# A decoder block on one core: another order of the beginning, and the state-space tables on VectorE

## The chip, the core and the metric

The kernel runs on one core of one Trainium2 chip. The core's engines work side by side and wait for one another by semaphores: TensorE (PE) multiplies matrices into PSUM, VectorE (DVE) and ScalarE (ACT) do element-wise work, GpSimd (POOL) too, and SyncE (SP) issues most DMA transfers. The metric is the device time of one execution in microseconds (us); lower is better.

## The reference

One layer of a hybrid decoder for 256 positions of 2048 channels, all in float32. What matters here, cut to the core:

```python
h = rms_norm(x, g_mix)
proj = h @ w_in                      # u, z_ssm, c_q, k, v, z_attn, k_idx, w_idx, gate_ssm, gate_attn
# state-space branch: 64 groups of 16 channels, a complex diagonal state of 64 per group
abar = exp(dt * (a_re + i a_im));  bb = f(abar) * b
h_t = abar * h_(t-1) + bb u_t;     y = Re(c h) + d_skip * u        # associative scan over positions
y_ssm = glu(gelu(y) @ w_glu) * silu(z_ssm)
# attention branch: an indexer picks 64 keys per query; attention over those keys
y_attn = attention(q(c_q), k, v, picked) * silu(z_attn)
merged = sigmoid(gate_ssm) * (y_ssm @ w_ssm_out) + sigmoid(gate_attn) * (y_attn @ w_attn_out)
x = x + merged @ w_o;  x = x + sigmoid(rms_norm(x) @ w_ple_gate) * rms_norm(p @ w_ple)
return rms_norm(x, g_final)
```

## The kernel before, in words

**Arithmetic.** Every matrix product is made of three passes on rounded parts. A weight `w` is split into `hi` (a cast on ScalarE, `unit_hi`, L243) and `lo` = `w` - `hi` (a subtraction on VectorE, `unit_lo`, L255); the activation has such parts too (`xgh`, `xgl` for x times the gain). A product is hi·high + hi·low + lo·high (`mm3`, L144), three matmuls for each of the 16 k-tiles of 128 channels.

**Units.** The weights stream from memory in units of 128 x 1024 (512 KB). The list `units` holds them in the order of their use: 16 units for u (8 blocks of two halves, `block_k16`, L280), 16 for z_ssm, 32 for gate_ssm, 16 for z_attn, 24 for gate_attn; unit 104 is the first of the query latent c_q, then come k (112 to 115), v, the query products, and from unit 132 the state-space output. A unit of u has 24 matmuls of 256 columns. `weave` (L296) swaps units 1 and 2, so that the first halves of the first two blocks (k-tiles 0 to 7) come before their second halves. A raw unit has 5 buffers, `hi` and `lo` have 4 each; `hi` of unit k waits until TensorE is done with unit k - 4.

**The step.** One turn of the last loop of `block_kernel` is a step, and its number is that of its unit. Step s emits, in this order: what the unit needs first (`need`), its matmuls, `unit_hi(s + 3)`, evictions that are due (`run_deferred`, L194), `unit_lo(s + 2)`, the load of a later unit (`issue_unit`, L88), and a portion of background work (`pump`, L229).

**Background work.** The tables of the state-space branch, the norm of x, the branch itself and the attention are Python generators (threads). `pump(BUDGET)` adds 1.3 to a credit (at most 3.0) and advances the first thread that is due until the credit is used; a thread names the charge of each piece in its `yield`, and `("lag", n)` lets it rest until n steps later. `drain` (L237) advances a thread to its end without looking at the credit. Threads are served in the order of the list.

- `s5_tables` (L754) builds the tables: `s5_small` (L681) some 60 instructions of 128 x 32, then four complex products of 128 x 1024 on VectorE (12 pieces at 1.14), then on GpSimd seven powers of abar (`s5_powers`, L732, 49 small instructions) and two more complex products (`cmul_g`), for which nothing is charged. Transposes on TensorE follow. It is spawned with lag 3.
- `s5_gen` (L819) is the branch: twice (halves of the channels) inputs by TensorE, then the scan on VectorE (L859, L861, L863, L865, 19 complex products of 4 instructions each, charge (66 + 32 n) / 960 + 0.05 apiece, n = 32 three times, 8 three times, 1 seven times, 7 three times, 31 three times: 41 in all), then outputs by TensorE. It starts when the tables are done. In a complex product L859 and L861 are independent, L863 adds the first to the target, L865 the second to the same target, and the next product reads that target.
- Unit 104 has `need=["s5"]`: `drain` of `s5_gen` ahead of its matmuls.
- `xnorm_gen` (L366) sums the squares of x: products on GpSimd in `xprep` (L364), one square on ScalarE, sums on GpSimd (L368 to L370) and VectorE, then a factor per position (`rstd_cols`, `row_of`) that the evictions of u (`ev_u`, L386) need.

**Who sets the order.** The framework keeps each engine's queue in the order in which it places the instructions: an instruction goes as soon as its inputs and its buffer are ready by the framework's own reckoning, and among the ready ones the one emitted first. On the chip every queue then runs strictly in that order.

**The beginning.** `first_loads` (L112) issues, all on SP's queue: the gains, x k-tiles 0 and 1, half of unit 0, x 2 and 3, the other half, x 4 to 7, unit 1, x 8 to 11, x 12 to 15, units 2 to 4, and the small table of the branch. Eighteen warm-up matmuls follow. `xprep(q)` makes the parts of four k-tiles of x (casts on ScalarE L360, low parts on VectorE L362) and, for q of 0 and 1, their squares on GpSimd; the second half of x is prepared by `late_x` (L396) ahead of unit 2. In `mm3` order the first block goes k-tile by k-tile through all three passes. The evictions of u run one step after their block, those of the first two blocks four steps after.

Of the kernel before, what the change touches and what calls it, by code (L numbers as in the profile page):

```python
# [18 lines left out]
P = 128  # L19
T = 256  # L20
# [8 lines left out]
GA1 = 3  # L29
NC = 4  # L30
CW = 512
NWARM = 18
BUDGET = 1.3
XLAG = 1
ULATE = 4
TRLAG = 2

C_U, C_ZS, C_CQ, C_K, C_V, C_ZA, C_KI, C_GS, C_GA = 0, 1024, 2048, 2560, 2816, 3072, 4096, 4176, 6224
# [6 lines left out]
def block_kernel(ctx: ExitStack, tc: tile.TileContext, A: dict, out: bass.AP):  # L45
# [18 lines left out]
    def slot(tag, shape, dt=F32):  # L64
        return cp.tile(shape, dt, tag=tag, name=nm(tag))
# [22 lines left out]
    def issue_unit(between=None):  # L88
        n = dma_next[0]
        if n >= len(units):  # L90
            return
        c, h, cols = units[n][:3]
        kind, idx = chunks[c]
        r = wp.tile([P, 1024], F32, tag="raw", name=nm("raw"), bufs=5)
        src = (A["wts"][idx] if kind == "w" else A["wvk"][idx])[:, h * cols:(h + 1) * cols]
        q = 2 if between else 1
        for i in range(q):
            s = slice(i * cols // q, (i + 1) * cols // q)
            nc.sync.dma_start(r[:, s], src[:, s])
            if between and i == 0:  # L100
                between()
        raws[n] = r
        dma_next[0] += 1
# [6 lines left out]
    sabc = const("sabc", [P, 3, 32])  # L110

    def first_loads():  # L112
        def xload(k, n):
            nc.sync.dma_start(xT[:, k:k + n, :], A["xT"][:, k:k + n, :])

        nc.sync.dma_start(gains, A["gains"])
        xload(0, 2)
        issue_unit(lambda: xload(2, 2))
        xload(4, 4)
        issue_unit()  # L120
        xload(8, 4)
        xload(12, 4)
        for i in range(3):
            issue_unit()
        nc.sync.dma_start(sabc, A["sabc"])
# [9 lines left out]
    mhalf = const("mhalf", [P, 2])  # L135
    V.memset(mhalf, -0.5)
    first = const("first", [P, 2])
    S.activation(first, mhalf, AF.Copy)


    def mm(o, l, r, start=True, stop=True, **kw):
# [70 lines left out]
    def spawn_first(gen):  # L212
        t = spawn(gen)
        threads.insert(0, threads.pop())
        return t
# [61 lines left out]
    def flush():  # L277
        run_deferred(True)

    def block_k16(act, evac, need=None, need1=None, M=P, acc=None, late=1):  # L280
        st = {}

        def go(h, hi, lo):
            ah, al = act()
            if h == 0:
                st["ps"] = (acc or main_ps)()
            ps = st["ps"]
            for k in range(8):
                kt = 8 * h + k
                mm3(ps[:M, :T], hi[:, k * M:(k + 1) * M], lo[:, k * M:(k + 1) * M], ah[:, kt, :], al[:, kt, :],  # L290
                    kt == 0, kt == 15)
            if h == 1:
                defer(late, lambda: evac(ps))
        return (lambda hi, lo: go(0, hi, lo), need), (lambda hi, lo: go(1, hi, lo), need1)
# [59 lines left out]

    xsq = slot("S2", [P, KT, T])

    def xprep(q):
        r = slice(4 * q, 4 * q + 4)
        for k in range(4 * q, 4 * q + 4):
            S.activation(xgh[:, k, :], xT[:, k, :], AF.Copy, scale=gcol(G_MIX, k))  # L360
        for k in range(4 * q, 4 * q + 4):
            STT(xgl[:, k, :], xT[:, k, :], gcol(G_MIX, k), xgh[:, k, :].bitcast(F32), ALU.mult, ALU.subtract)  # L362
        if q < 2:
            G.tensor_tensor(xsq[:, r, :], xT[:, r, :], xT[:, r, :], ALU.mult)  # L364

    def xnorm_gen():  # L366
        S.activation(xsq[:, 8:16, :], xT[:, 8:16, :], AF.Square)
        G.tensor_tensor(xsq[:, 0:4, :], xsq[:, 0:4, :], xsq[:, 4:8, :], ALU.add)  # L368
        G.tensor_tensor(xsq[:, 8:12, :], xsq[:, 8:12, :], xsq[:, 12:16, :], ALU.add)
        G.tensor_tensor(xsq[:, 0:4, :], xsq[:, 0:4, :], xsq[:, 8:12, :], ALU.add)  # L370
        yield ("lag", XLAG)
        TT(xsq[:, 0:2, :], xsq[:, 0:2, :], xsq[:, 2:4, :], ALU.add)
        TT(xsq[:, 0, :], xsq[:, 0, :], xsq[:, 1, :], ALU.add)
        yield 1.0
        yield ("lag", 1)
        R["col1"] = rstd_cols(xsq[:, 0, :], P, D, "r1")
        yield ("lag", 1)
        R["row1"] = row_of(R["col1"], "row1")
# [14 lines left out]
                R["s5"] = spawn(s5_gen(), 1)  # L393
        return f

    def late_x():  # L396
        xprep(2)
        xprep(3)
        R["xnorm"] = spawn_first(xnorm_gen())

    ua = {}

    def first_acc(nb):
# [4 lines left out]
        return f  # L408

    for nb in range(8):  # L410
        first = nb < 2
        add_chunk(*block_k16(xact, ev_u(nb), need1=[late_x] if nb == 0 else None,
                             acc=first_acc(nb) if first else None, late=ULATE if first else 1))
        if nb == 1:
            weave()

# [315 lines left out]
    def s5_powers():  # L732
        abr, abi = R["abar"][:, 0], R["abar"][:, 1]

        def cmul(i, xr, xi, yr, yi):
            t0, t1 = st_("er"), st_("eq")
            tt = G.tensor_tensor
            tt(t0, xi, yi, ALU.mult)
            tt(t1, xr, yr, ALU.mult)
            tt(pre[:, i], t1, t0, ALU.subtract)  # L740
            tt(t0, xr, yi, ALU.mult)
            tt(t1, xi, yr, ALU.mult)
            tt(psi[:, i, 1], t1, t0, ALU.add)
            G.tensor_scalar(psi[:, i, 0], psi[:, i, 1], -1.0, None, ALU.mult)

        cmul(0, abr, abi, abr, abi)
        for i, a, b in ((1, 0, 0), (2, 1, 0), (3, 1, 1), (4, 3, 3), (5, 4, 3), (6, 4, 4)):
            cmul(i, pre[:, a], psi[:, a, 1], pre[:, b], psi[:, b, 1])

    def bc(ap, n):  # L750
        return ap.unsqueeze(-1).to_broadcast(list(ap.shape) + [n])
# [2 lines left out]
    def s5_tables():  # L754
# [6 lines left out]
        ci = slot("S7", [P, 3, 32, 32])  # L761
        nc.sync.dma_start(ci[:, 0], A["sc"][:, 1])
        yield 0.0
        bb = slot("S1", [P, 2, 32, 2, 32])
# [6 lines left out]
            TT(o, o, ci[:, 1], op)  # L771
            yield 1.14

        def cmul_g(o, xr, xi, yr, yi, op):
            G.tensor_tensor(o, xr, bc(yr, 32), ALU.mult)
            G.tensor_tensor(ci[:, 2], xi, bc(yi, 32), ALU.mult)
            G.tensor_tensor(o, o, ci[:, 2], op)
# [5 lines left out]
        yield from cmul_v(Bi, bi, br, f[:, 0], f[:, 1], ALU.add)  # L783
        yield from cmul_v(bb[:, 0, :, 0, :], Br, Bi, abr, abi, ALU.subtract)
        yield from cmul_v(bb[:, 1, :, 0, :], Bi, Br, abr, abi, ALU.add)
        s5_powers()
        S.activation(ct[:, 1, 0], ci[:, 0], AF.Copy, scale=-1.0)
        cmul_g(ct[:, 0, 1], ct[:, 0, 0], ci[:, 0], abr, abi, ALU.subtract)
        cmul_g(ct[:, 1, 1], ct[:, 0, 0], ct[:, 1, 0], nabi, abr, ALU.add)
        bl = slot("S2", [P, 2, 16, P])  # L790
        yield ("lag", 2)
        for c in range(2):
# [295 lines left out]
    assert sum(1 for c in chunks if c[0] == "w") == NCH, (len(chunks), NCH)  # L1088


    R["s5t"] = spawn(s5_tables(), 3)
    first_loads()
    for i in range(NWARM):
        mm(wps[:, :T], warm[:, :P], warm)
    unit_hi(0)
    xprep(0)
    unit_lo(0)
    xprep(1)
    unit_hi(1)
    unit_lo(1)  # L1100
    unit_hi(2)
    NU = len(units)
    for s in range(NU):
        step[0] = s
# [130 lines left out]
```

## Time and profile before

| | us |
|---|---|
| runs | 813.30, 812.24, 811.18 |
| median | 812.24 |
| the profiled execution, its own time | 811.61 |
| its span in the profile | 809.8 |
| TensorE busy | 783.5 |
| VectorE busy | 575.1 |
| ScalarE busy | 393.9 |
| GpSimd busy | 72.7 |

The profile shows one execution. "Busy" is the time in which an engine executes; matmuls are pipelined, so their durations overlap and a start-to-start distance is what one costs. Line numbers such as L264 are those of the kernel; all matmuls have the helper's line, L142, and are told apart by their tiles (XH and XL are the parts of x, aux and main are PSUM). "Granted clock" is TensorE's, as a share of 2.4 GHz. A wait is named with the instruction or DMA that ended it.

### The profile page before, as it was taken

How to read it: one execution, taken by the hardware profiler on the slowest of the kernel's cores; microseconds unless marked ns; L12 is line 12 of the kernel's file. 1: busy time of each engine (PE TensorE's matmuls, PEld its weight loads, DVE VectorE, ACT ScalarE, POOL GpSimd, SP SyncE). 2: the span in 40 equal slices, each digit the busy share in tenths (PEclk: the TensorE clock that was granted, in tenths of full speed). 3: DMA queues.
4: the chain of work that ended last, by engine and by line, in shares of the span. 5: the costliest groups of instructions: out<-in, count | busy, mean ns of one | idle time of the engine just before them, and what ended most of it. 6: DMA issues, size and time to landing. Idle time of an engine off the chain costs nothing.

```text
span 809.8 us, 12802 instructions
## 1 busy us (share of the span) xinstructions
PE 783.5 (97%) x5020; PEld 676.5 (84%) x5020; DVE 575.1 (71%) x834; ACT 393.9 (49%) x536; POOL 72.7 (9%) x77
## 2 busy tenths in 40 slices
PE   6899999999999999999999999999999999999993
PEld 5899997887999887799999987887887888888882
DVE  6999656999645999664669877666688555556662
ACT  6354544544566454463445474535445444445542
POOL 4369900000000000000000000000000000000000
PEclk7999999999999999999999999999999999999997
DMA  8576854656745655734754546676767665555522
GB/s 288 182 261 193 270 192 141 201 177 210 260 135 176 194 184 182 252 121 129 243 183 156 194 162 226 224 238 199 268 202 236 224 204 185 184 182 181 184 79 104
DMA packets 52061, 158.07 MB, mean 195 GB/s; under 512 B 5920, under 2 KB 12064, under 8 KB 51616
## 3 DMA queue, kind: packets, MB, share of 16 engines
q1 hardware_dynamic: 47392, 150.96, 57.2%
q10 hardware_dynamic: 4608, 6.29, 2.2%
q8 instruction: 39, 0.64, 0.3%
q14 instruction: 22, 0.18, 0.1%
HBM read 147.79 MB, written 8.39 MB: 193 GB/s over the span
## 4 chain that ended last, share of the span: by engine, by line
PE 36%; issue 11%; DMA 1%; DVE 1%; ACT 1%; ACTq 0%; POOLq 0%; POOL 0%; DVEq 0%
PE main L142 33%; PE aux L142 2%; PE aux L150 1%; DMA zld<-za_d 1%; DVE lo L264 0%; ACT hi L252 0%; DMA raw<-in_wts_dram 0%; DVE S L1022 0%; ACT S L1127 0%; ACTq L1230 0%; ACT S L586 0%; DVE t L980 0%; POOLq L1230 0%; POOL r_c L633 0%; ACT S L1023 0%
## 5 line engine op out<-in xcount | busy, mean ns | idle before, releaser
L252 ACT CAST hi<-raw 128x1024 fp32r<-128x1024 f32 (+2 forms) x259 | 266.4, 1031 | 363.7 <-PE main L142 318.3
L264 DVE TENSOR_TENSOR lo<-raw,hi 128x1024 fp32r<-128x1024 f32 (+2 forms) x259 | 316.5, 1225 | 154.6 <-ACT hi L252 154.0
L142 PE MATMUL main<-hi,S 128*128 128x512 f32 x544 | 175.3, 397 | 0.9 <-ACT S L1023 0.9
L142 PE MATMUL main<-hi,XH 128*128 128x512 f32 (+1 forms) x416 | 163.1, 392 | 0.0
L142 PE MATMUL main<-lo,XH 128*128 128x512 f32 (+1 forms) x416 | 162.4, 390 | 0.4 <-DVE lo L264 0.4
L142 PE MATMUL main<-hi,XL 128*128 128x512 f32 (+1 forms) x416 | 161.9, 389 | 0.0
L142 PE MATMUL main<-XH,hi 128*128 128x256 f32 x448 | 127.5, 285 | 0.0
L142 PE MATMUL main<-XH,lo 128*128 128x256 f32 x448 | 126.2, 282 | 0.0
L142 PE MATMUL main<-XL,hi 128*128 128x256 f32 x448 | 126.1, 282 | 0.0
L142 PEld LDWEIGHTS main<-hi,S 128*128 128x128 f32 x544 | 102.2, 188 | 25.2 <-ACT S L1023 1.6
L142 PE MATMUL main<-lo,S 128*128 128x512 f32 x272 | 107.9, 397 | 0.0
L142 PEld LDWEIGHTS main<-lo,XH 128*128 128x128 f32 x416 | 78.1, 188 | 18.8 <-DVE lo L264 1.9
L142 PEld LDWEIGHTS main<-hi,XH 128*128 128x128 f32 x416 | 78.1, 188 | 18.0
L142 PEld LDWEIGHTS main<-hi,XL 128*128 128x128 f32 x416 | 78.1, 188 | 17.3
L142 PEld LDWEIGHTS main<-XH,hi 128*128 128x128 f32 x448 | 84.8, 189 | 0.6
L142 PEld LDWEIGHTS main<-XH,lo 128*128 128x128 f32 x448 | 84.8, 189 | 0.0
L142 PEld LDWEIGHTS main<-XL,hi 128*128 128x128 f32 x448 | 84.7, 189 | 0.0
L142 PE MATMUL main<-S,hi 128*128 128x256 f32 x384 | 69.3, 283 | 0.1
L142 PEld LDWEIGHTS main<-S,hi 128*128 128x128 f32 x384 | 58.9, 188 | 1.7 <-issue 1.0
L142 PEld LDWEIGHTS main<-lo,S 128*128 128x128 f32 x272 | 51.2, 188 | 11.0
L142 PE MATMUL main<-S,lo 128*128 128x256 f32 x192 | 53.8, 280 | 0.0
L142 PEld LDWEIGHTS main<-S,lo 128*128 128x128 f32 x192 | 36.2, 188 | 0.0
(213 smaller groups left out, 687.0 us busy)
## 6 DMA issues: line engine op xcount, KB each, us to landing
raw<-in_wts_dram SPq DMA_DIRECT2D x247, 512.0 KB, 4.0
raw<-in_wvk_dram SPq DMA_DIRECT2D x8, 336.0 KB, 2.9
gs_d<-big ACTq DMA_DIRECT2D x8, 256.0 KB, 3.9
ga_d<-big ACTq DMA_DIRECT2D x8, 256.0 KB, 4.0
big<-gs_d SPq DMA_DIRECT2D x8, 256.0 KB, 4.3
big<-ga_d SPq DMA_DIRECT2D x8, 256.0 KB, 3.8
S<-in_grow_dram SPq DMA_DIRECT2D x2, 1024.0 KB, 7.7
big<-in_xtok_dram SPq DMA_DIRECT2D x8, 256.0 KB, 3.9
```

The lines of the kernel that those rows point to most:

```text
L142: PE.matmul(o, l, r, start=start, stop=stop, **kw)
L150: PE.matmul(o, i, idn, is_transpose=True)
L252: S.copy(hi[:, o], src[:, o])
L264: TT(lo[:, o], src[:, o], his[u][:, o].bitcast(F32), ALU.subtract)
```

## The change

- Loads: the gains and x k-tiles 0 and 1 are issued on ScalarE's queue; the rest of x stays on SP's queue between the weight units. The first activation, which brings the table load with it, is emitted after these loads. Two more weight units are loaded ahead of the loop, so that step s issues unit s + 7 where it issued s + 5.
- Warm-up: 30 matmuls instead of 18.
- Order: the first two blocks run pass by pass (all eight hi·high, then lo·high, then hi·low of a half) instead of k-tile by k-tile. All of x is prepared ahead of the loop. The evictions of the first four blocks wait 6, 5, 3 and 2 steps.
- Squares and sums of x: two squares on ScalarE, four sums on VectorE, as a thread spawned with lag 2. Nothing of it on GpSimd.
- Tables: the powers and the last two complex products run on VectorE, and their pieces are charged (seven at 1.2, six at 1.14); the thread is spawned with lag 7.

```diff
-NWARM = 18
+NWARM = 30
-        nc.sync.dma_start(gains, A["gains"])
-        xload(0, 2)
-        issue_unit(lambda: xload(2, 2))
-        xload(4, 4)
+        nc.scalar.dma_start(gains, A["gains"])
+        xload(nc.scalar, 0, 2)
+        issue_unit(lambda: xload(nc.sync, 2, 2))
+        xload(nc.sync, 4, 4)
         issue_unit()
-        xload(8, 4)
-        xload(12, 4)
+        xload(nc.sync, 8, 4)
+        xload(nc.sync, 12, 4)
...
-            for k in range(8):
+            if split:
+                for i, (w, a) in enumerate(((hi, ah), (lo, ah), (hi, al))):
+                    for k in range(8):
+                        kt = 8 * h + k
+                        mm(ps[:M, :T], w[:, k * M:(k + 1) * M], a[:, kt, :], start=kt == 0 and i == 0,
+                           stop=kt == 15 and i == 2)
+            for k in range(0 if split else 8):
...
-        if q < 2:
-            G.tensor_tensor(xsq[:, r, :], xT[:, r, :], xT[:, r, :], ALU.mult)
     def xnorm_gen():
-        S.activation(xsq[:, 8:16, :], xT[:, 8:16, :], AF.Square)
-        G.tensor_tensor(xsq[:, 0:4, :], xsq[:, 0:4, :], xsq[:, 4:8, :], ALU.add)
-        G.tensor_tensor(xsq[:, 8:12, :], xsq[:, 8:12, :], xsq[:, 12:16, :], ALU.add)
-        G.tensor_tensor(xsq[:, 0:4, :], xsq[:, 0:4, :], xsq[:, 8:12, :], ALU.add)
-        yield ("lag", XLAG)
-        TT(xsq[:, 0:2, :], xsq[:, 0:2, :], xsq[:, 2:4, :], ALU.add)
-        TT(xsq[:, 0, :], xsq[:, 0, :], xsq[:, 1, :], ALU.add)
-        yield 1.0
+        for h in range(2):
+            S.activation(xsq[:, 8 * h:8 * h + 8, :], xT[:, 8 * h:8 * h + 8, :], AF.Square)
+            yield 0.0
+            yield ("lag", 1)
+        for n in (8, 4, 2, 1):
+            TT(xsq[:, 0:n, :], xsq[:, 0:n, :], xsq[:, n:2 * n, :], ALU.add)
+            yield 1.0
...
-        add_chunk(*block_k16(xact, ev_u(nb), need1=[late_x] if nb == 0 else None,
-                             acc=first_acc(nb) if first else None, late=ULATE if first else 1))
+        add_chunk(*block_k16(xact, ev_u(nb), acc=first_acc(nb) if nb < 2 else None,
+                             late=(6, 5, 3, 2)[nb] if nb < 4 else 1, split=nb < 2))
...
-            tt = G.tensor_tensor
+            tt = TT
...
-            G.tensor_scalar(psi[:, i, 0], psi[:, i, 1], -1.0, None, ALU.mult)
+            V.tensor_scalar(psi[:, i, 0], psi[:, i, 1], -1.0, None, ALU.mult)
         cmul(0, abr, abi, abr, abi)
+        yield 1.2
         for i, a, b in ((1, 0, 0), (2, 1, 0), (3, 1, 1), (4, 3, 3), (5, 4, 3), (6, 4, 4)):
             cmul(i, pre[:, a], psi[:, a, 1], pre[:, b], psi[:, b, 1])
+            yield 1.2
...
-        s5_powers()
+        yield from s5_powers()
         S.activation(ct[:, 1, 0], ci[:, 0], AF.Copy, scale=-1.0)
-        cmul_g(ct[:, 0, 1], ct[:, 0, 0], ci[:, 0], abr, abi, ALU.subtract)
-        cmul_g(ct[:, 1, 1], ct[:, 0, 0], ct[:, 1, 0], nabi, abr, ALU.add)
+        yield from cmul_v(ct[:, 0, 1], ct[:, 0, 0], ci[:, 0], abr, abi, ALU.subtract)
+        yield from cmul_v(ct[:, 1, 1], ct[:, 0, 0], ct[:, 1, 0], nabi, abr, ALU.add)
...
-    R["s5t"] = spawn(s5_tables(), 3)
+    R["xnorm"] = spawn(xnorm_gen(), 2)
+    R["s5t"] = spawn(s5_tables(), 7)
     first_loads()
+    S.activation(first, mhalf, AF.Copy)
...
     unit_hi(0)
-    xprep(0)
+    xhi(range(8))
     unit_lo(0)
-    xprep(1)
+    xlo(range(8))
     unit_hi(1)
     unit_lo(1)
     unit_hi(2)
+    xhi(range(8, 16))
+    xlo(range(8, 16))
+    for i in range(2):
+        issue_unit()
```

`xhi` and `xlo` are the casts and the low parts that `xprep` held.

## Rows read from the trace of the kernel before

**Rows 1.** The page's part 1: busy us, share of span, instructions.
```profile
PE 783.5 (97%) x5020; PEld 676.5 (84%) x5020; DVE 575.1 (71%) x834; ACT 393.9 (49%) x536; POOL 72.7 (9%) x77
```

**Rows 2.** Stretches: length, busy us by engine, clock, DMA share, GB/s.
```profile
35.00:100.00 65.00, 65.00 (x555) 65.00 (x554) 55.73 (x99) 32.40 (x41) 51.33 (x56) 1.00 0.78 249
345.00:797.00 452.00, 450.53 (x2482) 384.26 (x2482) 295.69 (x437) 221.88 (x324) 5.44 (x8) 1.00 0.58 188
```

**Rows 3.** The same for TensorE alone: three stretches of the beginning.
```profile
5.50:34.30 28.80, 20.26 (x120) 0.76 0.69 239
24.45:27.50 3.05, 0.00 (x0) 1.00 0.02 3
27.50:32.30 4.80, 4.78 (x27) 0.64 0.64 201
```

**Rows 4.** Timeline, SP and ScalarE: start, us, operation [idle before, releaser].
```profile
3.06 0.43 SPq L114 DMA_DIRECT2D S<-in_xT_dram  x1
...
9.30 0.62 ACT L252 CAST hi<-raw 128x512 fp32r<-128x512 f32 x1 [2.17 <-DMA raw<-in_wts_dram]
...
10.55 1.70 ACT L360 ACTIVATE XH<-S,gains 128x256 fp32r<-128x256 f32 x4 [0.63 <-DMA S<-in_xT_dram]
```

**Rows 5.** All engines in a stretch, columns as in rows 2.
```profile
10.00:15.00 5.00, 1.74 (x5) 1.01 (x4) 4.56 (x3) 4.45 (x11) 4.31 (x2) 0.50 1.01 392
```

**Rows 6.** Timeline, VectorE and GpSimd in the beginning.
```profile
10.59 1.89 POOL L364 TENSOR_TENSOR S<-S 128x1024 f32<-128x1024 f32 x1 [2.22 <-DMA S<-in_xT_dram]
...
11.09 4.97 DVE L362 SCALAR_TENSOR_TENSOR XL<-S,gains,XH 128x256 fp32r<-128x256 f32 x4 [0.44 <-ACT XH L360]
...
17.19 3.24 DVE L362 SCALAR_TENSOR_TENSOR XL<-S,gains,XH 128x256 fp32r<-128x256 f32 x8
...
19.40 4.51 POOL L369 TENSOR_TENSOR S<-S 128x1024 f32<-128x1024 f32 x1 [4.42 <-ACT S L367]
...
24.08 4.52 DVE L264 TENSOR_TENSOR lo<-raw,hi 128x1024 fp32r<-128x1024 f32 x2
```

**Rows 7.** Timeline, TensorE in the beginning.
```profile
1.04 4.02 PE L142 MATMUL main<-warm 128*128 128x256 bf16 x18 [1.04 <-DVE mhalf L136]
...
8.71 0.58 PE L142 MATMUL aux<-XL,hi 128*128 128x256 f32 x1 [1.17 <-DVE XL L362]
```

**Rows 8.** Timeline, GpSimd at the start, VectorE in the first scan.
```profile
0.86 0.95 POOL L805 MEMSET kb<- 128x1024 f32 x1
...
133.99 1.22 DVE L863 TENSOR_TENSOR S<-S,S 128x1024 f32<-128x1024 f32 x1
135.13 1.22 DVE L264 TENSOR_TENSOR lo<-raw,hi 128x1024 fp32r<-128x1024 f32 x1
136.27 1.22 DVE L865 TENSOR_TENSOR S<-S,S 128x1024 f32<-128x1024 f32 x1
137.41 1.23 DVE L264 TENSOR_TENSOR lo<-raw,hi 128x1024 fp32r<-128x1024 f32 x1
```

**Rows 9.** VectorE alone in a stretch of the second scan.
```profile
294.54:331.89 37.35, 36.84 (x58) 1.00 0.58 191
```

**Rows 10.** Groups by form, VectorE, 294.54:331.79: busy us, mean ns, idle.
```profile
L264 DVE TENSOR_TENSOR lo<-raw,hi 128x1024 fp32r<-128x1024 f32 x12 | 14.7, 1221 | 0.0
...
L859 DVE TENSOR_TENSOR S<-S,pre 128x992 f32<-128x992 f32 x3 | 3.6, 1189 | 0.0
...
L859 DVE TENSOR_TENSOR S<-S,pre 128x224 f32<-128x224 f32 x3 | 1.7, 570 | 0.0
```

**Rows 11.** Groups by form, VectorE, 348 to 372 us, query-latent evictions.
```profile
L448 DVE SCALAR_TENSOR_TENSOR S<-t,gains,S 128x256 fp32r<-128x256 f32 x4 | 1.9, 479 | 0.0
L441 DVE TENSOR_TENSOR t<-main,row 128x256 f32<-128x256 f32 x4 | 1.7, 425 | 1.9 <-PE main L142 1.9
L450 DVE TENSOR_TENSOR acc<-acc,t 128x256 f32<-128x256 f32 x3 | 1.3, 418 | 0.0
```

**Rows 12.** Timeline, ScalarE at the start of unit 89.
```profile
294.54 1.05 ACT L252 CAST hi<-raw 128x1024 fp32r<-128x1024 f32 x1 [1.02 <-PE main L142]
```

More of the change, by code (lines that the diff above doesn't have):

```diff
@@ L31 @@
 CW = 512
-NWARM = 18
+NWARM = 30
 BUDGET = 1.3
-XLAG = 1
-ULATE = 4
 TRLAG = 2
@@ L112, in first_loads, with xload @@
     def first_loads():
-        def xload(k, n):
-            nc.sync.dma_start(xT[:, k:k + n, :], A["xT"][:, k:k + n, :])
-        nc.sync.dma_start(gains, A["gains"])
-        xload(0, 2)
-        issue_unit(lambda: xload(2, 2))
-        xload(4, 4)
+        def xload(q, k, n):
+            q.dma_start(xT[:, k:k + n, :], A["xT"][:, k:k + n, :])
+        nc.scalar.dma_start(gains, A["gains"])
+        xload(nc.scalar, 0, 2)
+        issue_unit(lambda: xload(nc.sync, 2, 2))
+        xload(nc.sync, 4, 4)
         issue_unit()
-        xload(8, 4)
-        xload(12, 4)
+        xload(nc.sync, 8, 4)
+        xload(nc.sync, 12, 4)
         for i in range(3):
@@ L137, in block_kernel @@
     first = const("first", [P, 2])
-    S.activation(first, mhalf, AF.Copy)
     def mm(o, l, r, start=True, stop=True, **kw):
@@ L278, in flush, with block_k16 @@
         run_deferred(True)
-    def block_k16(act, evac, need=None, need1=None, M=P, acc=None, late=1):
+    def block_k16(act, evac, need=None, need1=None, M=P, acc=None, late=1, split=False):
         st = {}
@@ L355, in block_kernel, with xhi, xlo @@
     xsq = slot("S2", [P, KT, T])
-    def xprep(q):
-        r = slice(4 * q, 4 * q + 4)
-        for k in range(4 * q, 4 * q + 4):
+    def xhi(ks):
+        for k in ks:
             S.activation(xgh[:, k, :], xT[:, k, :], AF.Copy, scale=gcol(G_MIX, k))
-        for k in range(4 * q, 4 * q + 4):
+    def xlo(ks):
+        for k in ks:
             STT(xgl[:, k, :], xT[:, k, :], gcol(G_MIX, k), xgh[:, k, :].bitcast(F32), ALU.mult, ALU.subtract)
-        if q < 2:
-            G.tensor_tensor(xsq[:, r, :], xT[:, r, :], xT[:, r, :], ALU.mult)
     def xnorm_gen():
-        S.activation(xsq[:, 8:16, :], xT[:, 8:16, :], AF.Square)
-        G.tensor_tensor(xsq[:, 0:4, :], xsq[:, 0:4, :], xsq[:, 4:8, :], ALU.add)
-        G.tensor_tensor(xsq[:, 8:12, :], xsq[:, 8:12, :], xsq[:, 12:16, :], ALU.add)
-        G.tensor_tensor(xsq[:, 0:4, :], xsq[:, 0:4, :], xsq[:, 8:12, :], ALU.add)
-        yield ("lag", XLAG)
-        TT(xsq[:, 0:2, :], xsq[:, 0:2, :], xsq[:, 2:4, :], ALU.add)
-        TT(xsq[:, 0, :], xsq[:, 0, :], xsq[:, 1, :], ALU.add)
-        yield 1.0
+        for h in range(2):
[5 more added lines that the diff above has]
+            yield 1.0
         yield ("lag", 1)
@@ L394, in ev_u @@
         return f
[L396 to L399, printed above, removed]
     ua = {}
@@ L410, in block_kernel @@
     for nb in range(8):
-        first = nb < 2
-        add_chunk(*block_k16(xact, ev_u(nb), need1=[late_x] if nb == 0 else None,
-                             acc=first_acc(nb) if first else None, late=ULATE if first else 1))
+        add_chunk(*block_k16(xact, ev_u(nb), acc=first_acc(nb) if nb < 2 else None,
+                             late=(6, 5, 3, 2)[nb] if nb < 4 else 1, split=nb < 2))
         if nb == 1:
@@ L760, in s5_tables @@
         nc.sync.dma_start(ct[:, 0, 0], A["sc"][:, 0])
-        ci = slot("S7", [P, 3, 32, 32])
+        ci = slot("S7", [P, 2, 32, 32])
         nc.sync.dma_start(ci[:, 0], A["sc"][:, 1])
@@ L772, in cmul_v @@
             yield 1.14
[L774 to L777, printed above, removed]
         br, bi = bp[:, 0], bp[:, 1]
```

## The prediction

> **What bounds the kernel now.** I read the page's busy times first, then a table of busy time by stretch, then the order of work where TensorE stands still. TensorE is busy 783.5 of 809.8 us [rows 1], and behind the first 35 us it has next to no hole [rows 2]: 65.0 of 65.0 us and 450.5 of 452 us. So that engine sets the end, and there are two ways to move it: the time it loses before 35 us, and any new hole after it. Idle time of the other engines is worth nothing by itself.
>
> How much is lost in the beginning is read from the count. From 35 to 100 us 555 matmuls take 65 us [rows 2], 0.117 us each, so a weight unit (24 of them) takes 2.81 us. Between 5.5 and 34.3 us there are 120 matmuls, five units, 14.0 us of work in 28.8 us [rows 3]. Three things make up the 14.8 us: waits for the first blocks, a hole of 3.05 us at 24.45, and after it 4.8 us in which 27 matmuls ran at a mean granted clock of 0.64, 1.6 us more than 27 x 0.117.
>
> **The change part by part, first the beginning.**
> Loads: the fourth x load (k-tiles 4 to 7) was issued at 3.06 us, and its casts start at 10.55 when it has landed [rows 4]. Gains and the first x load go to ScalarE's queue, two issues of 0.43 us [rows 4] and their spacing, 0.9 us, fewer ahead of it, so it can land at 9.6 at the earliest, and at 10.55 if only the engines count, which are 1.01 busy at 392 GB/s from 10 to 15 us [rows 5]. I take 10.1. The Trainium skill (Trainium Kernel Development and Optimization, Key Constraints) says that loads of the SP and the ACT queue share the same 16 engines and that a second issuer saves issue time alone; by it, and the busy engines of that row agree, the landing stays nearer to 10.55, and the sum would lose about half a microsecond of its gain. ScalarE has nothing to do before the first x load lands, so its two issues and the later table load are costed at nothing; without that cover they would cost their own 0.9 us.
>
> Squares on GpSimd: the low parts of x on VectorE (L362) take 4.97 us for four while GpSimd squares beside them, and 3.24 us for eight without; two weight splits (L264) take 4.52 us beside GpSimd's sums, the first from 19.40 on [rows 6], where one takes 1.22 us undisturbed [rows 10]. That makes 1.24 against 0.41 us for one low part. All GpSimd work of the beginning is gone, so VectorE follows ScalarE at once. The squares go to ScalarE (two of 2048 columns, at most 8 x 0.425 = 3.4 us each) and the sums to VectorE (15 x 256 columns, some 4.6 us by the 1.22 us of a 1024-wide split, [rows 10]), from step 2 on; the row factor is asked for only in step 8, and the splits run some units ahead of TensorE, so I cost them at nothing; if that cover is gone they cost their own 4.6 us.
>
> Order by pass: the first eight matmuls of a block need no low part of x, so the two first units wait only for casts. ScalarE: casts of k-tiles 4 to 7 from 10.1, four at 0.425 (1.70 for four, [rows 4]), to 11.8. Then 16 matmuls of unit 0 and 24 of unit 1 are free. The warm-up of 30 takes 30 x 0.22 us (18 took 4.02) to about 7.7 us; the first real matmul of before came earlier, but could not go on. A wait of 1.17 us was enough in before to drop the clock: the matmul at 8.71 takes 0.58 us [rows 7]. I therefore take the first 3 us at half speed, 14 matmuls, and the other 26 at 0.117: 11.8 + 3.0 + 3.0 = 17.8 us for two units. Unit 2 needs the low parts of k-tiles 8 to 15 and its own split: ScalarE needs 1.05 + 3.4 + 1.05 us more after 11.8 (a unit's cast takes 1.05, [rows 12]) and VectorE 0.6 for half a split: 17.9, so 18.0. Units 2 to 4 follow without a hole: 18.0 + 8.4 = 26.4 us, where before has 34.3. **Gain 7.9 us**; 5.0 if all 40 matmuls run at half speed, 9.6 if none does.
>
> **The second part of the change is not in the beginning: the table work moved to VectorE delays the scan.** The planner charges background work by the step, 1.3 per unit. Counting its charges from the code: the tables start in step 7 instead of 3, and the seven power products (1.2 each) and six wide operations (1.14 each) that GpSimd did are now charged, 15.2 or twelve steps. The first half of the scan starts in step 50 instead of 35, the second in step 91 instead of 76 (its TensorE inputs stand in steps 87 to 90, and TensorE keeps its order). At step 104 the first query-latent unit demands that the branch is finished (its drain). Before, 39 of the second scan's 41 charge units were given out by then; now about 20 are. The rest is emitted at once, ahead of everything younger.
>
> What is that rest on the chip? Unit 89 of before, 15 steps back, starts at 294.54, where TensorE frees a weight buffer for ScalarE [rows 12]. From there to the scan's end at 331.9 VectorE is 36.8 of 37.35 us busy [rows 9], with 12 weight splits [rows 10] that start 1.14 us apart from what follows them [rows 8]. The scan's share is 37.3 - 12 x 1.14 = 23.6 us. So when TensorE starts unit 104, VectorE has 23.6 us of scan that now ranks above the splits of unit 106 and later. And it stands in a stage with VectorE evictions (0.42 + 0.48 + 0.42 us per two units, [rows 11]), where the gate units of before had none.
>
> Strict rank would starve TensorE: units 104 and 105 take 5.6 us, then it waits to 23.6, a loss of 18.0 us. But rank decides only among what is ready: the memset of L805, emitted in step 28, ran at 0.86 us, and the split of unit 39 (emitted in step 37) stands between the scan's L863 and its older L865 of step 36, the split of unit 40 behind that [rows 8]. Each product of the scan has two such gaps, behind L863 and behind L865. If n splits get in before the scan ends, with c us of evictions, the hole is 23.6 + 1.14 n + c - 2.81 (n + 2). The rest holds three products 224 wide, three 992 wide [rows 10] and narrower ones. In the narrow ones (10 us) the gaps are dense, and units 106 to 109 get their splits as fast as buffers come free. The three wide ones last 13 us and have six gaps; waiting for them are the splits and three evictions per two units, the latter older; I give two gaps to splits. n = 6, and five evictions of 0.42 make c = 2: 23.6 + 6.8 + 2.0 - 22.5 = 9.9 us. After it the clock must rise again, 1.6 us as behind the hole at 24.45 [rows 3]. **Loss 11.5 us**, between 0.6 (n = 12) and 19.6 (n = 0). Then the queue is empty, and the branch's results are not read before unit 132.
>
> The moved table work's own time on VectorE (about 15 us of charges) and the later queue position of SP's other loads (two units more ahead of them) meet a TensorE that is some units behind its buffers; zero to 2 us, I take zero.
>
> **Sum** against the profiled execution's 811.61 us, 0.63 below the median: 811.6 - 7.9 + 11.5 = 815.2 us.
>
> **The rivals.**
> 1. The gaps let nearly all splits through (n of 10 or more, loss 0.6 to 4 us): 811.6 - 7.9 + 2.5 = 806.2 us, faster. For it: both gaps of the product at 134 us were used [rows 8], and 12 splits got in between 294.5 and 331.9 [rows 10]. Against it: most of those 12 outranked the scan, and now evictions compete for the gaps. It decides when n reaches 9 or so.
> 2. Strict rank, no gap used: 811.6 - 7.9 + 19.6 = 823.3 us. Against it [rows 8].
> 3. The beginning gains only 5.0, because the clock stays at half for both first units and loads land no earlier: 818.1 us. For it: the mean clock from 5.5 to 34.3 us was 0.76 [rows 3]; against it: no stop of GpSimd's making is left after 11.8 us.
> 4. The beginning does all it can and the hole stays smaller: 811.6 - 9.6 + 8 = 810 us, no change.
>
> **How the numbers follow.** A measurement of this kernel can tell about 0.3% (2.4 us) from no change. Forecast case 0.52, its own range 811 to 819 (0.37 slower, 0.14 within, 0.01 faster); rival 1 0.27 (0.23 faster, 0.04 within); rival 2 0.09 and rival 3 0.07, both slower; rival 4 0.05, within. Together 0.24 faster, 0.23 within, 0.53 slower. The range leaves out the ends of rivals 1 and 2: 804.5 to 822.
>
> **What would show it.** In the profile of after: unit 4's last matmul near 26 us, no hole at 24; the low parts of x at 0.41 us each; the second scan's first instruction some 34 us later than before's (42 by steps less 8); several splits queued behind the scan's 992-wide instructions, and TensorE holes six or seven units behind unit 104 (between 340 and 370 us) that end on a weight split, about 10 us in all, with the clock at half behind them. If TensorE has no such hole, the step about rank and gaps was wrong and the time is near 805; if unit 4 ends past 29 us, the step on the clock was.

## The result and the profile after

The kernel after takes 823.35 us (median of four, 822.84 to 823.95) where before takes 812.77 (four, 811.18 to 813.96): ratio 1.0132 [1.0111, 1.0152], slower. Its profiled execution has 823.03 us, 11.4 more than the one of before (811.61). The forecast was 815.2 us (804.5 to 822): the side was right, the time lies beyond the range. A time called a single run has no interval; the runs of the kernel before range from 809.8 to 814.7 us.

The page's part 1 of after, against [rows 1]:

```profile
PE 784.9 (96%) x5032; PEld 677.6 (83%) x5032; DVE 575.3 (70%) x891; ACT 391.5 (48%) x534; POOL 8.4 (1%) x17
```

TensorE is as busy as before in a span 11.2 us longer. Where it stands is told by a table of TensorE alone by stretch, whose columns are those of [rows 3]:

```profile
5.50:26.00 20.50, 18.37 (x127) 0.92 0.88 320
300.00:340.00 40.00, 40.00 (x224) 1.00 0.57 185
340.00:380.00 40.00, 21.56 (x301) 0.74 0.23 67
359.25:366.70 7.45, 7.45 (x200) 0.80 0.30 90
370.88:375.92 5.04, 5.04 (x23) 0.50 0.00 0
```

127 matmuls are in by 26 us, where before had 120 by 34.3 [rows 3]; between 340 and 380 us nearly half of the time is lost, and the two short stretches in it, of which more below, ran at a granted clock of 0.80 and 0.50. The waits of TensorE (what it waited for: us in total, times, longest) name two pieces:

```profile
PE aux L139 <- DVE S L857: 14.3, 1, 14.3
PE main L139 <- DVE t L436: 4.2, 1, 4.2
```

L857 is the last addition of a product of the scan (before: L865), L436 the first step of a query-latent eviction (before: L441). The timeline of TensorE there (start, us, operation, idle before and its releaser):

```profile
327.78 0.28 PE L139 MATMUL main<-XH,hi 128*128 128x256 f32 x1
...
344.71 0.28 PE L139 MATMUL main<-XH,lo 128*128 128x256 f32 x1
359.25 1.08 PE L139 MATMUL aux<-S,S 128*32 128x128 f32 x16 [14.26 <-DVE S L857]
...
370.88 0.55 PE L139 MATMUL main<-XH,hi 128*128 128x256 f32 x1 [4.17 <-DVE t L436]
371.22 0.42 PE L139 MATMUL main<-XL,hi 128*128 128x256 f32 x1
...
375.92 0.29 PE L139 MATMUL main<-XH,lo 128*128 128x256 f32 x1
376.05 0.28 PE L139 MATMUL main<-XH,hi 128*128 128x256 f32 x1
```

And VectorE's at the same place (lines left out between):

```profile
329.18 1.22 DVE L261 TENSOR_TENSOR lo<-raw,hi 128x1024 fp32r<-128x1024 f32 x1
...
345.70 1.22 DVE L261 TENSOR_TENSOR lo<-raw,hi 128x1024 fp32r<-128x1024 f32 x1
...
351.25 1.21 DVE L261 TENSOR_TENSOR lo<-raw,hi 128x1024 fp32r<-128x1024 f32 x1
...
356.79 1.21 DVE L261 TENSOR_TENSOR lo<-raw,hi 128x1024 fp32r<-128x1024 f32 x1
357.92 1.18 DVE L857 TENSOR_TENSOR S<-S,S 128x992 f32<-128x992 f32 x1
359.03 1.21 DVE L261 TENSOR_TENSOR lo<-raw,hi 128x1024 fp32r<-128x1024 f32 x1
...
366.79 1.26 DVE L890 SCALAR_TENSOR_TENSOR t<-S,gains,aux 128x256 f32<-128x256 f32 x3 [6.55 <-PE aux L139]
...
370.31 0.75 DVE L436 TENSOR_TENSOR t<-main,row 128x256 f32<-128x256 f32 x2
```

Weight splits (L261) did get in between the scan's instructions: seven from 329.18 to 356.79. No eviction did: the first runs at 370.31, behind the branch's output multiplications (L890). So TensorE finished units 104 to 109 (from 327.78 to 344.99 us), three blocks in the three main PSUM buffers, had no buffer for a fourth, and next in its queue stood the branch's output matmuls, which need the scan's end (357.92 + 1.18 = 359.10). From 346.9 us on it was not a split that it lacked: by the order of units those that start at 345.70 and 351.25 are of units 110 and 111, and neither unit ran.

The account of the 11.4 us. ScalarE's rows show when TensorE was done with the last gate unit, 103, in after:

```profile
327.98 0.69 ACT L425 ACTIVATE big<-main,r_c 128x512 f32<-128x512 f32 x1 [0.71 <-PE main L139]
```

and in before:

```profile
337.13 0.69 ACT L430 ACTIVATE big<-main,r_c 128x512 f32<-128x512 f32 x1 [0.72 <-PE main L142]
```

The beginning is worth 9.15 us, and it is still there. Against it stand the waits of 14.26 and 4.17, 2.3 us because the 23 distances from 370.88 to 375.92 are 0.219 instead of 0.118 us (granted clock 0.50), and 1.1 because the branch's outputs take 7.4 us (359.25 to 366.70, clock 0.80), of which before needed 6.3 at full clock beside a stall of 1.59. That stall, for which the profile shows no releaser, is gone in after, and why is open. 14.3 + 4.2 + 2.3 + 1.1 - 1.6 - 9.15 = 11.1 of 11.4 us.

### The profile page after: what moved, and what is told of

It reads as the page before. It is cut to its first block, busy times and chain, and to the rows that moved or that the text cites. A ratio compares the mean times of both kernels' runs of the same rounds, so it can differ in the third digit from the quotient of the medians.

```text
span 821.0 us, 12810 instructions
## 1 busy us (share of the span) xinstructions
PE 784.9 (96%) x5032; PEld 677.6 (83%) x5032; DVE 575.3 (70%) x891; ACT 391.5 (48%) x534; POOL 8.4 (1%) x17
## 4 chain that ended last, share of the span: by engine, by line
PE 36%; issue 11%; DMA 1%; DVE 1%; ACT 1%; ACTq 0%; POOLq 0%; POOL 0%; DVEq 0%
PE main L139 33%; PE aux L139 2%; PE aux L147 1%; DMA zld<-za_d 1%; DVE lo L261 0%; ACT hi L249 0%; DMA raw<-in_wts_dram 0%; DVE S L1014 0%; ACT S L1125 0%; ACTq L1228 0%; ACT S L581 0%; DVE t L972 0%; POOLq L1228 0%; POOL r_c L628 0%; ACT S L1015 0%
## 5 line engine op out<-in xcount | busy, mean ns | idle before, releaser
L261 DVE TENSOR_TENSOR lo<-raw,hi 128x1024 fp32r<-128x1024 f32 (+2 forms) x259 | 310.2, 1200 | 177.8 <-ACT hi L249 177.6
```

What stands on the lines that cost most here:

```text
L261: TT(lo[:, o], src[:, o], his[u][:, o].bitcast(F32), ALU.subtract)
```

## The experiments

Two theories stood against each other for the loss: the **count of steps** (charged table pieces and a later start delay the scan, and the drain at unit 104 finds its rest open) and the **engine** (VectorE has some 15 us more to do). A third, the **slots**, is about the size of the hole: the branch's output tiles (yv, yf, L889 and L891) share the tag "t" with its 9 buffers with the evictions' temporaries, and the slots of a tag go out in the order of emission, so an eviction emitted behind the drained outputs waits for theirs.

**The slots.** The outputs get a tag of their own:

```diff
-                yv = etmp("t", bufs=9)
+                yv = etmp("ty", bufs=4)
-                yf = etmp("t", bufs=9)
+                yf = etmp("ty", bufs=4)
```

and every other `etmp("t", bufs=9)` becomes `bufs=5`.

> Kernel after, with one edit: the eight output tiles of the state-space branch (yv, yf) get a tag of their own, 'ty' with 4 buffers, and 't', which they shared with the evictions' temporaries, has 5 instead of 9; the number of steps by which the scan is late stays. Theory (slots): in the kernel after, the query-latent evictions did not run before the branch's outputs because they take slots of the same tag behind them in program order. Then here the first query-latent eviction (t L436) starts ahead of the branch's output multiplication (L890), inside the scan, the main PSUM buffers come free one by one, TensorE's wait of 14.3 us at 344.9 on the scan's last instruction becomes shorter, by what the prediction gave for splits and evictions in the gaps (9.9 us hole), and the time is some 813 to 817 us. Rival (rank): the evictions are held back by the scan's older instructions whatever their slots; then t L436 still starts behind 366 us and the time stays at 823.

814.43 us, ratio 1.0024 [1.0014, 1.0035] to before. VectorE's and TensorE's timelines in this kernel:

```profile
341.45 0.46 DVE L436 TENSOR_TENSOR t<-main,row 128x256 f32<-128x256 f32 x1
...
351.51 0.47 DVE L436 TENSOR_TENSOR t<-main,row 128x256 f32<-128x256 f32 x1
```

```profile
352.13 0.55 PE L139 MATMUL main<-XH,hi 128*128 128x256 f32 x1 [5.44 <-DVE t L436]
...
357.58 0.58 PE L139 MATMUL main<-XH,lo 128*128 128x256 f32 x1 [4.68 <-DVE lo L261]
```

The evictions moved into the gaps of the scan, and the 18.4 us of waits became 5.44 + 4.68 + 0.35. Shown: in the kernel after it was the shared tag that held the evictions back, not the scan's older rank. With it out of the way the hole has the forecast's size (10.5 for 9.9 us), but only its second part ends on a weight split; the first, 5.44 us, ends on an eviction, which frees a PSUM buffer.

**The count against the engine.** The table work stays on VectorE, uncharged and started at step 3:

```diff
-        yield 1.2
+        yield 0.0
...
-            yield 1.2
+            yield 0.0
-        yield from cmul_v(ct[:, 0, 1], ct[:, 0, 0], ci[:, 0], abr, abi, ALU.subtract)
+        for _ in cmul_v(ct[:, 0, 1], ct[:, 0, 0], ci[:, 0], abr, abi, ALU.subtract):
+            pass
...
-    R["s5t"] = spawn(s5_tables(), 7)
+    R["s5t"] = spawn(s5_tables(), 3)
```

> Kernel after, with the table arithmetic still on VectorE, but given out in one go without a charge in the planner (as GpSimd's was in the kernel before) and the tables started at step 3 instead of 7. The scan then starts at the steps it had in the kernel before, 15 steps earlier than in the kernel after. Theory (count of steps): what cost the time is only that the scan's rest is still open when TensorE starts unit 104; so there is no hole behind unit 109, and the gain of the beginning stays: 823.4 less about 20 us (14.3 and 4.2 us of waits, some 3 of clock, less the 1.6 us of issue idle that the kernel before had), 803 to 805 us. Rival (engine): VectorE's load grew by some 15 us by the table work and this makes the scan late, however the steps are counted; then the hole stays at more than 8 us and the time above 812.

802.74 us, ratio 0.9884 [0.9861, 0.9907]: faster than both kernels. There is no hole; the longest wait of TensorE behind the warm-up is 0.9 us, and in the stretch in which after lost 18.4 us it is busy throughout:

```profile
340.00:380.00 40.00, 40.00 (x323) 1.00 0.50 149
```

The second scan starts at 257.18 us, 35.3 us or some twelve and a half units ahead of after's (292.52), not the fifteen steps that were expected: the sums of squares on VectorE are still charged at 4.0 instead of 1.0, which at 1.3 a step is 2.3 steps (worked out, not tried), and these do no harm. The reverse puts the arithmetic back on GpSimd and keeps charges and start:

```diff
-            tt = TT
+            tt = G.tensor_tensor
...
+        def cmul_g(o, xr, xi, yr, yi, op):
+            G.tensor_tensor(o, xr, bc(yr, 32), ALU.mult)
+            yield 1.14
...
-        yield from cmul_v(ct[:, 0, 1], ct[:, 0, 0], ci[:, 0], abr, abi, ALU.subtract)
+        yield from cmul_g(ct[:, 0, 1], ct[:, 0, 0], ci[:, 0], abr, abi, ALU.subtract)
...
```

> Kernel after, with the table arithmetic (powers and the two complex products) back on GpSimd, while the charges in the planner and the start at step 7 stay as in the kernel after. It is the reverse of the run without charges. Theory (count of steps): the scan is as late as in the kernel after, TensorE stands some 14 us behind unit 109, and the time is 821 to 825 us. Rival (engine): VectorE is relieved of about 15 us of work, the hole closes to less than 6 us and the time is below 812.

831.6 us (a single run). TensorE's waits here:

```profile
PE aux L139 <- DVE S L865: 14.3, 1, 14.3
PE main L139 <- DVE t L436: 4.2, 1, 4.2
PE main L139 <- DVE lo L261: 4.0, 4, 2.6
```

The two waits of after are there to the tenth (L865 is the last addition in this kernel), with VectorE relieved: the count decides, the engine theory falls. The 8.2 us above after were in no theory (821 to 825 us was the forecast). They lie between 26 and 100 us, where TensorE is busy 70.11 of 74.00 us at a mean granted clock of 0.95 (74.00 at 1.00 in after): a split waits beside GpSimd's 1024-wide products, as the two engines' timelines show:

```profile
78.88 3.37 POOL L776 TENSOR_TENSOR S<-S,S 128x1024 f32<-128x1024 f32 x1
```

```profile
79.93 3.40 DVE L261 TENSOR_TENSOR lo<-raw,hi 128x1024 fp32r<-128x1024 f32 x1
```

The rule of the Trainium skill (SBUF — State Buffer, Who interferes with whom) is that a VectorE instruction with two SBUF inputs and a GpSimd instruction that reads SBUF exclude each other, the later one standing until the earlier is through. The split ends 1.1 us after GpSimd's product, about one split's own time, so the rows agree.

**The size of the delay.** Tables started five steps later:

```diff
-    R["s5t"] = spawn(s5_tables(), 7)
+    R["s5t"] = spawn(s5_tables(), 12)
```

> Kernel after, with the tables started at step 12 instead of 7: five steps later, nothing else. Theory (count of steps): the scan's open rest at unit 104 grows by five steps of 1.3 charge units, 6.5 units, which were about 1.03 us each (23.6 us for 22.3 to 23 units), so TensorE's wait of 14.3 us on the scan grows to about 21 us and the time to 829 to 831 us. Rival: what TensorE waits for behind unit 109 does not scale with the start of the tables; then the time stays within 2 us of 823.

832.67 us (a single run), and of TensorE's waits:

```profile
PE aux L139 <- DVE S L857: 23.4, 1, 23.4
```

That is 9.1 us more than in after, where 6.5 charge units were to give about 7. The direction holds; the price by the unit does not. The scan starts 14.0 us later (306.55 instead of 292.52, five steps), but it ends only 9.2 us later (368.26 instead of 359.10), since it takes 61.7 us instead of 66.6: 14 splits stand between its instructions instead of 18. So a delay of the scan in this stage cost its time less the splits that were then done ahead of it, not its charges.

**The drain.** The branch is demanded at unit 112 instead of 104:

```diff
-        add_chunk(*block_k16(xact, ev_cq(nb), need=["s5"] if nb == 0 else None))
+        add_chunk(*block_k16(xact, ev_cq(nb)))
-        add_chunk(*block_k16(xact, ev_k(nb)))
+        add_chunk(*block_k16(xact, ev_k(nb), need=["s5"] if nb == 0 else None))
```

> Kernel after, with the drain of the state-space branch moved from unit 104 to unit 112: the first key unit demands it, no longer the first query-latent unit. Nothing is charged or started otherwise, so the scan has the same 15 steps of delay. Theory (drain and slots): by unit 112 eight more steps of 1.3 have been given out, so that some 15 of the 25.5 charge units are open, and the query-latent evictions are emitted ahead of the branch's outputs, so they take their slots first and run in the gaps of the scan. Then TensorE's waits behind unit 109 are below 5 us and the time is 804 to 812 us, with the same work on VectorE. Rival (the delay itself costs): TensorE has to stand until the scan's last instruction at 359 us wherever the drain is; then some 8 to 14 us of wait stay and the time is 815 to 823.

809.41 us, ratio 0.9965 [0.9951, 0.9979]. The waits are 6.3 us (0.86, 1.89 and 3.55), a little more than expected, all on weight parts; the first query-latent eviction runs inside the scan, with the tag still shared:

```profile
339.49 0.42 DVE L436 TENSOR_TENSOR t<-main,row 128x256 f32<-128x256 f32 x1
```

The scan is as late as in after (it starts at 293.20 and ends at 365.37), so the delay alone does not set the loss: where the drain stands, and with it what is emitted behind the outputs, does.

**Each part alone.** First the tables' part on top of before:

```diff
-            tt = G.tensor_tensor
+            tt = TT
...
-        s5_powers()
+        yield from s5_powers()
-        cmul_g(ct[:, 0, 1], ct[:, 0, 0], ci[:, 0], abr, abi, ALU.subtract)
+        yield from cmul_v(ct[:, 0, 1], ct[:, 0, 0], ci[:, 0], abr, abi, ALU.subtract)
...
-    R["s5t"] = spawn(s5_tables(), 3)
+    R["s5t"] = spawn(s5_tables(), 7)
```

> Kernel before, with the part of the tables alone (arithmetic on VectorE, charged, start at step 7), and the beginning of the kernel before. Theory (two independent parts): the scan is as late by steps as in the kernel after, the hole behind unit 109 is the same 14.3 and 4.2 us, and nothing is gained in the beginning: 812.6 + some 20 = 831 to 834 us. Rival (the parts interact): the earlier beginning of the kernel after had itself moved TensorE closer to the scan; with a TensorE that comes 9 us later the hole is 5 to 9 us shorter and the time 823 to 827.

831.98 us (a single run), with the two waits of after (L867 and L441 are the lines here):

```profile
PE aux L142 <- DVE S L867: 14.3, 1, 14.3
PE main L142 <- DVE t L441: 4.2, 1, 4.2
```

The beginning has no share in the hole; a later TensorE does not shorten it, since the scan is placed by steps and moves with it: it starts 35.3 us ahead of unit 104 here (300.18 and 335.44) as in after (292.52 and 327.78). The other way round, the kernel after with these lines as they were before:

> Kernel before, with the beginning of the kernel after and the tables as they were before (GpSimd, without charge, start at step 3). Theory (two independent parts): no hole behind unit 109, the gain of 9 us of the beginning stays: 803 to 805 us. Rival (GpSimd beside VectorE): in the kernel with the charged tables on GpSimd a weight split beside GpSimd took 2.8 to 3.4 us instead of 1.23 and TensorE lost 4 us between 26 and 100 us; if that also holds without charges, TensorE waits for low parts there and the time is 806 to 810.

803.1 us, ratio 0.9884 [0.9861, 0.9906]. The whole gain stays without the tables' part, and GpSimd's uncharged products cost nothing that the time shows, although single splits take up to 2.81 us there too; why the same products cost 8.2 us when they are charged is open. The parts add up within the noise: -9.6 and +19.3 give +9.7 of the 10.6 measured.

**Which part of the beginning.** On top of the uncharged kernel (802.74), one part undone at a time. The squares and first sums of x on GpSimd again:

```diff
-        for h in range(2):
-            S.activation(xsq[:, 8 * h:8 * h + 8, :], xT[:, 8 * h:8 * h + 8, :], AF.Square)
-            yield 0.0
-            yield ("lag", 1)
-        for n in (8, 4, 2, 1):
+        S.activation(xsq[:, 8:16, :], xT[:, 8:16, :], AF.Square)
+        yield 0.0
+        yield ("lag", 1)
+        G.tensor_tensor(xsq[:, 0:4, :], xsq[:, 0:4, :], xsq[:, 4:8, :], ALU.add)
+        G.tensor_tensor(xsq[:, 8:12, :], xsq[:, 8:12, :], xsq[:, 12:16, :], ALU.add)
+        G.tensor_tensor(xsq[:, 0:4, :], xsq[:, 0:4, :], xsq[:, 8:12, :], ALU.add)
+        yield ("lag", 1)
+        for n in (2, 1):
...
     xhi(range(8))
+    for r in (slice(0, 4), slice(4, 8)):
+        G.tensor_tensor(xsq[:, r, :], xT[:, r, :], xT[:, r, :], ALU.mult)
```

> Base is the kernel with the uncharged tables on VectorE (802.7 us). One part of the beginning is undone: the squares of x's k-tiles 0 to 7 and the first sums of squares run on GpSimd again. Theory (GpSimd beside VectorE): while GpSimd squares, one low part of x takes 1.24 instead of 0.41 us, and splits beside its sums take more than 2 us, as in the kernel before; the low parts of k-tiles 2 to 7 take up to 5 us longer, unit 0's last pass starts 3 to 5 us later, and the time is 805 to 808 us. Rival: the low parts are ahead of TensorE by enough to hide it, time within 1 us of 802.7.

815.02 us, ratio 1.0017 [0.9998, 1.0036]: no faster than before, and 7 us beyond the upper end of what was expected. VectorE's and GpSimd's timelines:

```profile
7.18 3.70 DVE L366 SCALAR_TENSOR_TENSOR XL<-S,gains,XH 128x256 fp32r<-128x256 f32 x2 [1.52 <-ACT XH L362]
10.80 2.85 DVE L261 TENSOR_TENSOR lo<-raw,hi 128x512 fp32r<-128x512 f32 x1
...
17.15 7.50 DVE L366 SCALAR_TENSOR_TENSOR XL<-S,gains,XH 128x256 fp32r<-128x256 f32 x8
```

```profile
6.62 1.89 POOL L1097 TENSOR_TENSOR S<-S 128x1024 f32<-128x1024 f32 x1 [4.47 <-DMA S<-in_xT_dram]
8.70 1.89 POOL L1097 TENSOR_TENSOR S<-S 128x1024 f32<-128x1024 f32 x1 [0.19 <-DMA S<-in_xT_dram]
10.68 2.42 POOL L372 TENSOR_TENSOR S<-S 128x1024 f32<-128x1024 f32 x1
```

In after two low parts take 0.88 us, a half split 0.69. Here they take 3.70 and 2.85 and end 0.3 and 0.55 us, about their own time, behind the ends of GpSimd's instructions (10.59, 13.10). The cast that waits for unit 4 starts at 34.7 us instead of 25.5. So five GpSimd instructions, put back, take away the whole gain of 9.2 with all other parts of the beginning in place; the other 3 us of the 12.3 are mostly a stall of 2.64 us among the branch's output matmuls (0.31 in the base), whose releaser the profile doesn't show, and which stays open.

The gains and the first x load on SP's queue again:

```diff
-        nc.scalar.dma_start(gains, A["gains"])
-        xload(nc.scalar, 0, 2)
+        nc.sync.dma_start(gains, A["gains"])
+        xload(nc.sync, 0, 2)
```

> Base is the kernel with the uncharged tables on VectorE (802.7 us). One part of the beginning is undone: gains and the first x load are issued on SP's queue ahead of the others again, none on ScalarE's. Theory: every later load on SP is issued 0.9 us later, k-tiles 4 to 7 land up to 1 us later than in the kernel after (8.7 us), unit 0's first pass ends up to 1 us later, and the time is 0.5 to 1.5 us longer: 803 to 804.5. Rival: the landing of the x loads is set by the transfers and not by their issue, or TensorE waits at that point for the low parts anyway: time within 0.4 us of 802.7.

804.08 us, ratio 0.9897 [0.9871, 0.9924]. Unit 0's second pass starts at 11.76 us instead of 10.93 and unit 1 at 15.17 instead of 13.82: this part is worth 1.3 us, as the times say too. Eighteen warm-up matmuls again:

```diff
-NWARM = 30
+NWARM = 18
```

> Base is the kernel with the uncharged tables on VectorE (802.7 us). One part of the beginning is undone: 18 warm-up matmuls instead of 30. They then end near 4 us instead of 6 to 7, TensorE stands some 2.9 us until the first block at 6.9. Theory: the clock is granted at half when the first passes run, so that the 24 matmuls of unit 0 take 0.21 us each until it rises; unit 1 starts up to 2 us later and the time is 803.5 to 805 us. Rival: unit 0's passes wait for casts and low parts anyway and the clock rises in them as it does with 30: within 0.5 us of 802.7.

802.91 us, ratio 0.9884 [0.9852, 0.9916]: no difference to the base. TensorE waits 2.01 us for the first block and then has eight matmuls every 0.95 us from 13.84 on, as with thirty (13.82). What TensorE's clock did in both is told in the last section. The first two units k-tile by k-tile again:

```diff
-                             late=(6, 5, 3, 2)[nb] if nb < 4 else 1, split=nb < 2))
+                             late=(6, 5, 3, 2)[nb] if nb < 4 else 1, split=False))
```

> Base is the kernel with the uncharged tables on VectorE (802.7 us). One part of the beginning is undone: the first two units go k-tile by k-tile again, three products each, instead of pass by pass. Theory: the order by pass lets TensorE run its first matmuls (6.88 to 10.9 us) before low parts of x are there; without it unit 0 starts when the first low part stands, near 11 us, ends between 14 and 16 instead of 13.8, and the time is 0 to 2.5 us longer, plus up to 1 us for a clock that rises later: 803 to 806 us. Rival: the order by pass is what carries most of the beginning's gain; then the time is above 808.

> The kernel of b_order (uncharged tables on VectorE, the first two units k-tile by k-tile), now timed against the kernel before, since one look put it at 801.65 us where its base had 802.74 (802.33 to 803.8). Theory (the order by pass earns nothing): the low parts of x follow the casts so closely once GpSimd is silent that k-by-k gives TensorE its work as early; the clock need not fall in the wait for k-tiles 2 to 7 that the order by pass has after two matmuls; 801 to 802.5 us, faster than all kernels so far. Rival: the one look was a lucky clock; 802.5 to 804 us, and the order by pass is neutral.

801.65 us in a single run, where 803 to 806 was expected; 802.31 as the median of four (802.09 to 802.57, ratio 0.9869 [0.985, 0.9888]), the lowest of all kernels, though its range overlaps that of its base (802.33 to 803.8): the order by pass earns nothing. Unit 0 does not wait until 11 us: it starts at 6.92 and unit 1 at 11.61, since once GpSimd is silent the low parts follow the casts closely enough. TensorE in this kernel and, below it, in the base:

```profile
9.80:13.00 3.20, 3.20 (x26) 1.00 1.01 410
```

```profile
9.80:13.00 3.20, 3.20 (x13) 0.50 1.03 417
```

K-tile by k-tile twice the matmuls run in this stretch, but TensorE then waits 1.2 us for unit 2's cast, and unit 4 ends at 25.17 us instead of 25.42.

## Why the prediction was wrong

**The beginning held, a little better than costed:** 9.15 us by the end of the gate units for 7.9 [rows 3]. Unit 4's end came at 25.7, not 26.4; low parts take 0.41 us each, as taken from their eight in [rows 6]. K-tiles 4 to 7 landed earlier than the 10.1 us of the sum: ScalarE runs the six casts of k-tiles 2 to 7 in one go, where before the last four began at 10.55 [rows 4]:

```profile
8.13 2.51 ACT L362 ACTIVATE XH<-S,gains 128x256 fp32r<-128x256 f32 x6
```

The engines are as full as in [rows 5] (1.02, 417 GB/s). By the Trainium skill's rule (Trainium Kernel Development and Optimization, Key Constraints) a second issuer saves issue time alone; the half microsecond that the prediction feared to lose by it was not lost, and the run with the loads back on SP's queue puts 1.3 us on the place in the queue. Unit 2 starts at 17.17 us, ahead of the 18.0 of the sum, which had it wait for low parts of k-tiles 8 to 15: units 2 and 3 are the second halves of the first two blocks and run pass by pass too, so their first eight matmuls need only casts. That bound also stands against the 9.6 us of gain for the case that no matmul runs at half speed; with it the case gives 7.9. What I gave to the order by pass and the warm-up, the runs give to the squares that left GpSimd.

**The clock term was near in size and not shown in its reason.** I took 3.0 us at half speed, from one wait of 1.17 us before a matmul of 0.58 us [rows 7]. The clock did fall there (1.00 from 7.0 to 7.5 us, 0.50 from 8.7 on), but the wait was not the first in before. In after the granted clock is 1.00 through waits of 1.07 and 0.97 us at 6.9 and 8.7 us and 0.50 from 10.8 to 14.0, while TensorE works; in before it is 1.00 over the hole of 3.05 us [rows 3] and falls only behind it. No run shows that such a wait by itself brings the clock down.

**The delay held.** The second scan's first instruction in before and in after:

```profile
259.45 1.23 DVE L859 TENSOR_TENSOR S<-S,pre 128x1024 f32<-128x1024 f32 x1 [0.57 <-ACT S L846]
```

```profile
292.52 1.22 DVE L851 TENSOR_TENSOR S<-S,pre 128x1024 f32<-128x1024 f32 x1
```

It comes 33.1 us later; some 34 were forecast. From 327.8, when TensorE starts unit 104, to the scan's end at 359.1 VectorE needs 31.3 us: less seven splits at 1.14 [rows 8] 23.3 for the scan, where the sum had 23.6 [rows 9, 10]. And n, the splits that get in, is 7 for the assumed 6.

**The step that failed is the next one:** "If n splits get in before the scan ends, with c us of evictions, the hole is 23.6 + 1.14 n + c - 2.81 (n + 2)", with c = 2 for five evictions in the gaps. It let the splits alone limit TensorE. With the seven splits that got in, and no eviction (c = 0), it would give 6.3 us. But without an eviction the limit is the three main PSUM buffers, six units, however many splits are ready: 31.3 less six units of 2.84 us here leaves 14.3, and 14.26 was measured. The evictions then follow the branch's outputs instead of running beside them, another 4.17. Waits of 18.4 for 9.9 and a clock at half behind them (3.4 us, the 2.3 and 1.1 above, for 1.6) make 21.8 where the loss was put at 11.5. The sum took the evictions for instructions that only need VectorE and their PSUM tile; that they take a slot of a tag which drained outputs had taken up it did not ask. With a tag of its own for the outputs the hole is 10.5 us. That this is near the formula's 9.9 is in part luck: 5.44 of it ended on an eviction, for which the formula has no wait. Its lower bound is off as well: for n = 12 it gives no hole (23.6 + 13.7 + 2.0 - 39.3 = 0), and the loss there was put at 0.6.

**The rivals.** Rival 2, no gap used, has nearly the measured time (823.3) by a mechanism that did not happen: seven gaps were used by splits, and the hole ended on the scan for want of a PSUM buffer. Rivals 1, 3 and 4 fell with the hole's size and the beginning's gain. The moved table work's own time, costed at nothing, is nothing: uncharged on VectorE the time is 802.74 us, on GpSimd 803.1.

**The sum with the measured terms:** 811.6 - 9.15 + 18.4 + 3.4 - 1.6 (the stall that is gone) = 822.7 us for 823.0.

## What to carry to other kernels

Where background work is emitted by charges, moving a piece to another engine means two things, the engine's time and its place in the count; here the first was worth nothing and the second 19 us. When emitted work outranks what follows, ask of the younger instructions which slot, bank or buffer they share with it: here one shared tag held every eviction behind the outputs, while seven splits slipped through. And count how far TensorE gets by its scarcest buffer, not by the one the argument is about.

## What the runs showed of the hardware

- Beside a GpSimd instruction VectorE stood: two low parts took 3.70 instead of 0.88 us, a half split 2.85 instead of 0.69, a whole one 3.40 instead of 1.23. I had priced this from [rows 6] as a factor of three; by the ends of the rows above it is a wait for the end of GpSimd's instruction.
- The longer warm-up is worth less than I took. With 30 of its matmuls the granted clock (the uncharged kernel) is 1.00 from 6.9 to 9.7 us, where TensorE's matmuls follow ScalarE's casts, 0.40 us apart at the closest, and 0.50 from 9.8 to 13.0, where from 10.9 on they start 0.213 us apart; from 13.2 on it is 1.00 again. With 18 the matmuls start 0.213 us apart from 10.78 to 13.13, the distance of the half clock, and 0.118 from 13.5 on. (The view prints a clock of 1.00 there, but this run's record of the clock begins only at 13.39 us.) So the longer warm-up's full clock fell into a time paced by casts; in both runs most of what followed of unit 0 ran at half, and unit 1 ran at full from 13.8 us on.
